# Layer norm and second norm: 1 / rms kept in the PSUM banks of its sums, Newton step in place, EPS added to the sum of squares

## The chip, the cores and the metric

The kernel runs on one core of one Trainium2 chip. The metric is the device time of one execution in microseconds (us); several runs are compared by their median. All times here are from the hardware profile of one execution or from those runs. The engines are named as the profile names them: PE (TensorE, the matmuls), DVE (VectorE), ACT (ScalarE), POOL (GpSimd) and SP (the queue that issues the loads).

## The reference, cut to what matters

One layer over 1088 tokens (1024 of a prompt, 64 of a decode step), 1024 channels, all float32. The change is in the layer norm inside it and in the second RMS norm:

```python
def layernorm(x, g, b):
    xf = x.astype(jnp.float32)
    mu = jnp.mean(xf, axis=-1, keepdims=True)
    xc = xf - mu
    var = jnp.mean(xc * xc, axis=-1, keepdims=True)
    r = xc * lax.rsqrt(var + EPS) * g.astype(jnp.float32) + b.astype(jnp.float32)
    return r.astype(x.dtype)

def layer(x, hist_a, hist_b, ...):
    h = rmsnorm(x, g_mix)
    z = jnp.einsum('btd,dc->btc', h, w_in)
    b_gate, c_gate, v, glu_val, glu_gate = jnp.split(z, 5, axis=-1)
    conv_a, new_a = causal_dwconv(c_gate * v, hist_a, conv_a_w)
    y_a = b_gate * conv_a
    u_b = glu_val * jax.nn.sigmoid(glu_gate)
    conv_b, new_b = causal_dwconv(u_b, hist_b, conv_b_w)
    y_b = jax.nn.silu(layernorm(conv_b + conv_b_bias, ln_b_g, ln_b_b))
    x = x + jnp.einsum('btc,cd->btd', jnp.concatenate([y_a, y_b], axis=-1), w_out)
    h2 = rmsnorm(x, g_ffn)
    f = jax.nn.silu(jnp.einsum('btd,df->btf', h2, w_gate)) * jnp.einsum('btd,df->btf', h2, w_up)
    x = x + jnp.einsum('btf,fd->btd', f, w_down)
    return x, new_a, new_b
```

## The kernel before

Channels lie on the 128 partitions and tokens on the free dimension. Each float32 matmul operand is split into two float16 parts (`high` L260 on ACT, `low` L263 on DVE or POOL; for weights `split_w`, L221 and L223 on ACT with L222 on POOL or L224 on DVE), and each product is three float16 matmuls (L247). Work is recorded as a list of tasks, each of which is a matmul group into two PSUM banks and its evacuation. Every engine runs its own instructions strictly in the order in which the recording wrote them, so an instruction that waits holds up everything behind it on its engine.

From about 225 us to 375 us of the span the kernel goes through these tasks:

- the last input projection tasks. The gate of group A is evacuated by L828, then split by L260 and L263; its convolution sums are made on POOL by L819.
- `layer_norm`, for two halves s of the tokens (every tile is 128x544: 2 x 272 tokens). L865 to L867 add up the four channel blocks. Matmuls with a matrix of ones (`column_sums`, L272) put the column sums into the PSUM tile `stat`, on every partition. L876 subtracts the mean, L878 squares, L880 adds the squares, and L272 sums again. Then `rstd_steps`: y0 on ACT (L289), m = mean square + EPS on ACT (L290), and three DVE instructions of one Newton step (L293, L294, L295). L896 multiplies the four blocks by the result r, L897 applies silu, L898 and L903 split.
- `out_task`: the output projection, 8 column blocks b for s = 0 and 8 for s = 1, evacuated into the residual `xt` by L942. L959 squares the result on ACT and L964 adds the squares.
- `second_norm`: for each s column sums (L272), y0, m and Newton as above, then eight products with r (L1003), each split by L260 and L263 into operands of the gate and up projections.
- gate and up projections (L1128 and L1131 evacuate the first ones). The first sums of weights for Strassen's scheme (L412, L413, L419, L423) are made on POOL.

PSUM in this stretch: three pairs of banks for products, and one pair, `stat`, that the six column sums use one after the other. r, m, y0 and t1 are tiles of the pool `sm` (11 buffers, names with s).

What the page calls L247 <-u,v or <-u,whl in this stretch are the output projection and the gate and up projections. w_o and w_gu are loads of weights that SP issues (L206) once their buffer is free.

Of the kernel before, what the change touches and what calls it, by code (L numbers as in the profile page):

```python
# [9 lines left out]
AF = mybir.ActivationFunctionType  # L10
ALU = mybir.AluOpType

P = 128
D = 1024
KB = D // P
GW = 512
# [12 lines left out]
EPS = 1e-6  # L29
# [6 lines left out]
ASC = 4.0  # L36
# [81 lines left out]
def halves(ap):  # L118

    return ap.rearrange("p (h w) -> p h w", h=2)  # L120


def quarter(ap, s):

    return halves(ap)[:, :, s * CW : (s + 1) * CW]
# [3 lines left out]
def trunk(ctx, tc, x, par, sta, stb, w_in, w_o, w_gu, w_ds, w_dl, y, st_out):  # L129
    nc = tc.nc  # L130
    pe, act, dve, gps = nc.tensor, nc.scalar, nc.vector, nc.gpsimd
# [15 lines left out]
    def nm(s):  # L147
        cnt[0] += 1
        return f"{s}{cnt[0]}"

    def unit(shape, dt=F32):
        return upool.tile(shape, dt, tag="u", name=nm("u"))
# [5 lines left out]
    def small():  # L158
        return sm.tile([P, HT], F32, tag="s", name=nm("s"))
# [10 lines left out]
    def begin(name, turns):  # L170

        cut_banks(part_b, "b", "ps_" + name)
        psum["phase"], psum["turns"], psum["n"] = name, turns, 0
# [16 lines left out]
    def stat_banks():  # L190
        if psum["phase"] == "rest":
            return bank2()
        if psum["phase"] == "first":
            return psum["b"].tile([P, 1, 512], F32, tag="stat", name=nm("stat"), bufs=2)
        return psum["b"].tile([P, 2, 512], F32, tag="stat", name=nm("stat"))

    def prm(i):
        return par_t[:, i : i + 1]
# [66 lines left out]
    def column_sums(parts):  # L265

        st = stat_banks()
        if len(parts[0].shape) == 3:
            n = parts[0].shape[2]
            for h in range(2):  # L270
                for i, p in enumerate(parts):
                    pe.matmul(  # L272
                        st[:, h, :n], ones, p[:, h], start=i == 0, stop=i == len(parts) - 1
                    )
            return st[:, :, :n]
        n = parts[0].shape[1]
        for i, p in enumerate(parts):
            pe.matmul(st[:, 0, :n], ones, p, start=i == 0, stop=i == len(parts) - 1)
        return st[:, 0, :n]

    def like(ap, t):

        return t[:, : ap.shape[1]] if len(ap.shape) == 2 else halves(t[:, : 2 * ap.shape[2]])

    def rstd_steps(sums, inv_n, scale, tiles=None):


        m, y0, t1, r = tiles or (like(sums, small()) for _ in range(4))
        act.activation(y0, sums, AF.Abs_reciprocal_sqrt, bias=epst[:, 0:1], scale=inv_n)  # L289
        act.activation(m, sums, AF.Identity, bias=epst[:, 0:1], scale=inv_n)  # L290

        def newton():
            dve.scalar_tensor_tensor(t1, m, -0.5 * scale, y0, ALU.mult, ALU.mult)  # L293
            dve.tensor_tensor(t1, t1, y0, ALU.mult)  # L294
            dve.scalar_tensor_tensor(r, t1, 1.5 * scale, y0, ALU.add, ALU.mult)  # L295
            return r

        return newton

    def rstd_of(sums, inv_n, scale):  # L300
        return rstd_steps(sums, inv_n, scale)()


    xt = cst.tile([P, KB, T], F32, name="xt")
# [32 lines left out]
    def run(steps):  # L337
        for _ in steps:
            pass
# [6 lines left out]
    for s, b in [(0, b) for b in range(KB)] + [(1, b) for b in ORDER1]:  # L346
# [5 lines left out]
        r, o, e = len(raws) - 1, (b % 2) * 1024, len(entries)  # L352
# [35 lines left out]
    scaled, loaded, sums = set(), {}, {}  # L388
# [449 lines left out]
    for j in range(NJ):  # L838
        for q, hf in TRIPLE:
# [3 lines left out]
                lambda acc, j=j, hf=hf, fn=fn: fn(acc, j, hf),  # L843
# [7 lines left out]
    def layer_norm():  # L851
        run(taps.steps)
        run(staps.steps)
        for j in range(NJ):
            act.activation(
                cb[j][:, TP:].rearrange("p (b t) -> p b t", b=SB),
                sacc[:, j],
                AF.Identity,
                bias=prm(PBI + j),
            )  # L860
        yb.extend(unit([P, 2, T], F16) for _ in range(NJ))
        for s in range(2):
            c = [quarter(b, s) for b in cb]
            tot = halves(small())
            dve.tensor_tensor(tot, c[0], c[1], ALU.add)  # L865
            dve.tensor_tensor(tot, tot, c[2], ALU.add)
            dve.tensor_tensor(tot, tot, c[3], ALU.add)  # L867
            got = []

            def first(tot=tot, s=s, c=c, got=got):  # L870
                if s == 0:
                    begin("out", "aab")
                mean = column_sums([tot])
                sq = []
                for j in range(NJ):
                    dve.scalar_tensor_tensor(c[j], mean, -1.0 / GW, c[j], ALU.mult, ALU.add)  # L876
                    sq.append(halves(small()))
                    act.activation(sq[j], c[j], AF.Square)  # L878
                for j in range(1, NJ):
                    dve.tensor_tensor(sq[0], sq[0], sq[j], ALU.add)  # L880
                got.append(sq[0])

            midway.append((PART1[s], first))
            while len(got) < 1:
                yield

            def second(got=got):
                got.append(rstd_steps(column_sums(got), 1.0 / GW, 1.0))

            midway.append((PART2[s], second))  # L890
            while len(got) < 2:
                yield
            r = got[1]()
            hl = [[quarter(yb[j][:, i], s) for i in range(2)] for j in range(NJ)]
            for j in range(NJ):
                dve.tensor_tensor(c[j], c[j], r, ALU.mult)  # L896
                act.activation(c[j], c[j], AF.Silu, scale=prm(PLG + j), bias=prm(PLB + j))  # L897
                act.activation(hl[j][0], c[j], AF.Copy, scale=ASC)  # L898
                if j == 1:
                    yield  # L900
            yield
            for j in range(NJ):
                dve.scalar_tensor_tensor(hl[j][1], c[j], ASC, hl[j][0], ALU.mult, ALU.subtract)  # L903
            ln_done.add(s)
            yield
# [5 lines left out]
    def out_task(b, s, *bg, part=None):  # L911
# [28 lines left out]
        def post(acc):  # L940
            o = quarter(xt[:, b], s)
            dve.scalar_tensor_tensor(o, acc[:, :, :CW], IN_SC, o, ALU.mult, ALU.add)  # L942
            return add_square((1, s), b, s)
# [9 lines left out]
    ssum, rstd2 = {}, {}  # L953
    ops = {}

    def add_square(key, b, s):

        sq = halves(small())
        act.activation(sq, quarter(xt[:, b], s), AF.Square)  # L959
        if key not in ssum:  # L960
            ssum[key] = sq
            return None
        o = ssum[key]
        return lambda: dve.tensor_tensor(o, o, sq, ALU.add) and None  # L964

    def operand(name, kp):

# [4 lines left out]
    def put(name, u, s, t):  # L972
        hl = [quarter(ops[name][u][:, i], s) for i in range(2)]
        high(hl[0], t)
        pend.append((hl[1], t, hl[0]))

    def settle(n):
        while len(pend) > n:
            low(*pend.pop(0))
# [3 lines left out]
    def second_norm(s):  # L983

        got = []


        def sums():
            got.append(rstd_steps(column_sums([ssum[1, s]]), 1.0 / D, ASC))

        midway.append((PART3, sums))
        while not got:
            yield
        r = got[0]()
        for name in ("B11", "B12", "B21", "B22"):
            if name not in ops:
                ops[name] = [unit([P, 2, T], F16) for _ in range(2)]
        for u in range(2):
            for q in range(2):
                tq = tqs[s, u, q] = (unit if (s, u, q) == (0, 0, 0) else unit_v)([P, 2, 2, CW])  # L1000
                for kk in range(2):
                    k = 4 * q + 2 * u + kk
                    dve.scalar_tensor_tensor(  # L1003
                        tq[:, kk], quarter(xt[:, k], s), prm(PG2 + k), r, ALU.mult, ALU.mult
                    )
                for hf in range(2):
                    put(f"B{q + 1}{hf + 1}", u, s, tq[:, :, hf])
                settle(2)
                yield
        settle(0)  # L1010
        yield
# [492 lines left out]
```

## Time and profile before

| | |
|---|---|
| median of 3 runs | 1020.53 us (1019.23 to 1020.68) |
| time of the profiled execution | 1019.75 us |
| its span in the profile | 1018.0 us |
| PE busy | 986.4 us (97%) |
| DVE busy | 761.1 us (75%) |
| ACT busy | 385.8 us (38%) |
| POOL busy | 340.6 us (33%) |

The span is the time from the first to the last recorded instruction; the 1.75 us beside it are outside the records. PE is nearly always busy, so a change can move the end only where PE stands still, or by work that PE does. The granted clock of TensorE was 0.996 of full speed over the span.

### The profile page before, as it was taken

Reading aid. Unit: us, or ns where it says so; the run is one execution under the profiler, and the core shown is the slowest. Engines: PE = TensorE matmul, PEld = TensorE weight load, DVE = VectorE, ACT = ScalarE, POOL = GpSimd, SP = SyncE. Lnnn points to the kernel's source line nnn. Section 1 sums busy time; section 2 is a strip of 40 time slices with the busy share of each in tenths; the row PEclk is TensorE's granted clock in tenths of the full one; section 3 lists DMA queues with packets and bytes.
Section 4 is the critical chain, followed back from the end, with each engine's and each line's share of the span. In section 5 each row is a group of like instructions: output and inputs, shape, how many; then the busy total and the mean of one; then the engine's idle time right before and its main releaser. Section 6 shows DMA issues by size and latency. Waiting matters only on the chain.

```text
span 1018.0 us, 19624 instructions
## 1 busy us (share of the span) xinstructions
PE 986.4 (97%) x8482; PEld 829.8 (82%) x8482; DVE 761.1 (75%) x1067; ACT 385.8 (38%) x692; POOL 340.6 (33%) x279
## 2 busy tenths in 40 slices
PE   5999999999899999999999999999999999999995
PEld 4788888888788878888888888888888888888884
DVE  7949999997677678987776767777676677755548
ACT  6611133237463534443322444332244333223332
POOL 3487854544000015323133322323422413240033
PEclk9999999999999999999999999999999999999998
DMA  9021111111410111121112112011211101211104
GB/s 345 32 83 43 42 43 53 42 43 53 166 42 1 43 42 42 43 73 33 36 69 84 43 42 73 32 62 46 80 43 53 62 32 63 82 44 42 42 1 176
DMA packets 17031, 63.01 MB, mean 62 GB/s; under 512 B 1169, under 2 KB 8481, under 8 KB 12081
## 3 DMA queue, kind: packets, MB, share of 16 engines
q1 hardware_dynamic: 16896, 61.67, 17.4%
q8 instruction: 66, 1.08, 0.5%
q14 instruction: 21, 0.16, 0.1%
q0 software_dynamic: 48, 0.09, 0.0%
HBM read 56.71 MB, written 5.05 MB: 61 GB/s over the span
## 4 chain that ended last, share of the span: by engine, by line
PE 68%; DVE 25%; ACT 3%; issue 2%; DMA 1%; POOL 0%; DVEq 0%; ACTq 0%
PE two L247 63%; DVE cv L548 12%; PE one L247 4%; DVE xt L1371 1%; DVE whl L224 1%; DVE u L263 1%; DVE v L1003 1%; DMA wf<-w_o 1%; DVE s L295 1%; PE stat L272 1%; DVE h L263 1%; DVE s L294 1%; DVE cv L543 1%; DVE v L263 1%; DVE xt L1319 0%
## 5 line engine op out<-in xcount | busy, mean ns | idle before, releaser
L247 PEld LDWEIGHTS <-whl 128*128 128x128 f16 x7464 | 730.2, 98 | 140.1 <-issue 4.5
L247 PE MATMUL two<-u,whl 128*128 128x272 f16 x4416 | 523.7, 279 | 3.8 <-DVE u L263 2.9
L247 PE MATMUL two<-h,whl 128*128 128x272 f16 x1512 | 186.1, 279 | 0.0
L247 PE MATMUL two<-v,whl 128*128 128x272 f16 x1536 | 178.5, 279 | 0.0
L423 POOL TENSOR_TENSOR s<-wf,s 128x512 f32<-128x512 f32 (+1 forms) x32 | 46.9, 1467 | 382.0 <-DVE whl L224 382.0
L223 ACT ACTIVATE whl<-wf 128x512 f16<-128x512 f32 (+1 forms) x150 | 87.6, 589 | 143.0 <-PE two L247 141.0
L548 DVE SCALAR_TENSOR_TENSOR cv<-u,par_t,cv 128x1024 f32<-128x1024 f32 x116 | 139.7, 1281 | 0.0
L224 DVE SCALAR_TENSOR_TENSOR whl<-wf,whl 128x512 f16<-128x512 f32 (+1 forms) x150 | 112.3, 765 | 1.2 <-ACT whl L223 1.2
L1278 DVE SCALAR_TENSOR_TENSOR xt<-two,xt 128x544 f32<-128x544 f32 x108 | 75.7, 719 | 41.0 <-PE two L247 40.4
L1169 DVE SCALAR_TENSOR_TENSOR s<-two,s 128x544 f32<-128x544 f32 x40 | 28.9, 723 | 66.1 <-PE two L247 66.1
L412 POOL TENSOR_TENSOR s<-wf 128x512 f32<-128x512 f32 (+1 forms) x32 | 40.6, 1270 | 111.8 <-DVE u L263 97.5
L223 ACT ACTIVATE whl<-s 128x512 f16<-128x512 f32 (+1 forms) x96 | 55.4, 583 | 59.5 <-PE two L247 55.8
L224 DVE SCALAR_TENSOR_TENSOR whl<-s,whl 128x512 f16<-128x512 f32 (+1 forms) x96 | 65.5, 696 | 0.0
L247 PE MATMUL two<-u,v 128*128 128x272 f16 x480 | 56.3, 279 | 1.9 <-DVE xt L942 1.9
L247 PEld LDWEIGHTS <-v 128*128 128x128 f16 x480 | 47.0, 98 | 11.1 <-issue 2.1
L260 ACT ACTIVATE h<-s 128x544 f16<-128x544 f32 x52 | 34.0, 657 | 52.8 <-DVE s L1162 48.1
L247 PE MATMUL one<-v,u 128*128 128x272 f16 (+2 forms) x480 | 49.2, 267 | 1.9 <-DVE v L263 1.8
L247 PEld LDWEIGHTS <-u 128*128 128x128 f16 x480 | 42.8, 104 | 8.7 <-issue 2.6
L1203 DVE SCALAR_TENSOR_TENSOR s<-two,s 128x544 f32<-128x544 f32 x20 | 14.5, 724 | 45.2 <-PE two L247 45.2
L222 POOL TENSOR_TENSOR whl<-wf,whl 128x512 f16<-128x512 f32 x38 | 44.1, 1187 | 10.1 <-ACT whl L221 10.0
L419 POOL TENSOR_TENSOR wf<-wf 128x512 f32<-128x512 f32 (+1 forms) x32 | 46.6, 1457 | 0.0
L413 POOL TENSOR_TENSOR s<-s,wf 128x512 f32<-128x512 f32 (+1 forms) x32 | 41.5, 1296 | 2.5
(127 smaller groups left out, 749.8 us busy)
## 6 DMA issues: line engine op xcount, KB each, us to landing
wf<-w_gu SPq DMA_DIRECT2D x22, 1024.0 KB, 4.9
wf<-w_ds SPq DMA_DIRECT2D x12, 768.0 KB, 4.2
wf<-w_in SPq DMA_DIRECT2D x8, 1024.0 KB, 5.1
wf<-w_o SPq DMA_DIRECT2D x6, 1024.0 KB, 5.3
xt<-x SPq DMA_DIRECT2D x3, 1088.0 KB, 11.3
y<-xt SPq DMA_DIRECT2D x2, 1088.0 KB, 5.1
u<-w_in SPq DMA_DIRECT2D x4, 512.0 KB, 7.7
wf<-w_dl SPq DMA_DIRECT2D x2, 1024.0 KB, 4.8
```

The source lines that it names most:

```text
L222: return whl, lambda: gps.tensor_tensor(lo, wf, hi, ALU.subtract) and None
L223: act.activation(hi, wf, AF.Copy, scale=WSC)
L224: return whl, lambda: dve.scalar_tensor_tensor(lo, wf, WSC, hi, ALU.mult, ALU.subtract) and None
L247: pe.matmul(out, w_[:, wpart, col : col + P], hl[:, apart, t0 : t0 + out.shape[1]], start=first and (i, q) == one, stop=last and (i, q) == ...
L260: act.activation(hi, tmp, AF.Copy)
L263: eng.tensor_tensor(lo, tmp, hi, ALU.subtract)
L412: gps.tensor_tensor(s1, a21, a22, ALU.add)
L413: gps.tensor_tensor(s2, s1, a11, ALU.subtract)
L419: gps.tensor_tensor(a21, a11, a21, ALU.subtract)
L423: gps.tensor_tensor(src, a12, src, ALU.subtract)
L548: dve.scalar_tensor_tensor(o_, i_, w, c, ALU.mult, ALU.add)
L1278: dve.scalar_tensor_tensor(o, bk[a_][:, :, :CW], IN_SC, o, ALU.mult, ALU.add)
```

## The change: what it does

`rstd_steps` is still there for the final norm. The layer norm and the second norm, in both halves, call a new function `rstd_kept`. It has one ACT instruction, y0 from the raw sums (the scale 1/n is in the activation), and no m. The Newton step runs on the PSUM tile of the sums, in place, and r stays there: `stat` is held until the last product with r. EPS no longer enters with y0 and m; it is added, times n / 128, to the partial sums of squares by the first of the adds, which becomes a scalar_tensor_tensor in place of a tensor_tensor (`add_with`).

```diff
-    def rstd_of(sums, inv_n, scale):
-        return rstd_steps(sums, inv_n, scale)()
+    def rstd_kept(sums, inv_n, scale):
+
+        y0 = like(sums, small())
+        act.activation(y0, sums, AF.Abs_reciprocal_sqrt, scale=inv_n)
+
+        def newton():
+            dve.scalar_tensor_tensor(sums, sums, -0.5 * scale * inv_n, y0, ALU.mult, ALU.mult)
+            dve.tensor_tensor(sums, sums, y0, ALU.mult)
+            dve.scalar_tensor_tensor(sums, sums, 1.5 * scale, y0, ALU.add, ALU.mult)
+            return sums
+
+        return newton
+
+    def add_with(eps, o, sq):
+
+        if eps:
+            dve.scalar_tensor_tensor(o, o, eps, sq, ALU.add, ALU.add)
+        else:
+            dve.tensor_tensor(o, o, sq, ALU.add)
...
-                    dve.tensor_tensor(sq[0], sq[0], sq[j], ALU.add)
+                    add_with(EPS * GW / P if j == 1 else None, sq[0], sq[j])
...
-                got.append(rstd_steps(column_sums(got), 1.0 / GW, 1.0))
+                got.append(rstd_kept(column_sums(got), 1.0 / GW, 1.0))
...
-            ssum[key] = sq
+            ssum[key] = sq, []
             return None
-        o = ssum[key]
-        return lambda: dve.tensor_tensor(o, o, sq, ALU.add) and None
+        o, others = ssum[key]
+        others.append(b)
+        eps = EPS * D / P if len(others) == 1 else None
+        return lambda: add_with(eps, o, sq)
...
-            got.append(rstd_steps(column_sums([ssum[1, s]]), 1.0 / D, ASC))
+            got.append(rstd_kept(column_sums([ssum[1, s][0]]), 1.0 / D, ASC))
```

In the changed kernel the lines are numbered 17 to 19 higher behind the new functions: L293 to L295 become L306 to L308, L289 becomes L303, L828 L845, L896 L913, L897 L914, L942 L959, L1003 L1022, L412 L429, L413 L430, L419 L436; the adds of squares L880 and L964 become L316 (the first of each row of adds, with EPS) and L318.

On DVE, at the layer norm of half 0, before (u are the channel blocks, s the tiles of the pool `sm`, two a product in PSUM; the numbers are those of the recording):

```order
L293 SCALAR_TENSOR_TENSOR s_2862<-s_2860,s_2861 128x544
L294 TENSOR_TENSOR s_2862<-s_2862,s_2861 128x544
L295 SCALAR_TENSOR_TENSOR s_2863<-s_2862,s_2861 128x544
L896 TENSOR_TENSOR u_1771<-u_1771,s_2863 128x2x272
L896 TENSOR_TENSOR u_1773<-u_1773,s_2863 128x2x272
L828 SCALAR_TENSOR_TENSOR s_2808<-two_2908,s_2808 128x544
```

and the same place now:

```order
L306 SCALAR_TENSOR_TENSOR stat_2857<-stat_2857,s_2860 128x2x272
L307 TENSOR_TENSOR stat_2857<-stat_2857,s_2860 128x2x272
L308 SCALAR_TENSOR_TENSOR stat_2857<-stat_2857,s_2860 128x2x272
L913 TENSOR_TENSOR u_1771<-u_1771,stat_2857 128x2x272
L913 TENSOR_TENSOR u_1773<-u_1773,stat_2857 128x2x272
L845 SCALAR_TENSOR_TENSOR s_2808<-two_2904,s_2808 128x544
```

No instruction of DVE changed its place; each of these now reads one tile from PSUM and one from SBUF, where it read two from SBUF.

On POOL, behind the last layer norm work, before (the sums of weights for Strassen's scheme, with the engines and queues whose counts each waits for):

```order
L222 TENSOR_TENSOR v_3024<-wf_2600,v_3024 128x1024 [waits DMAHW3_49,DVE_49,Activation_49]
L412 TENSOR_TENSOR s_4383<-wf_3993 128x512 [waits DVE_49,DMAHW6_49,PE_49,Pool_49]
L413 TENSOR_TENSOR s_4384<-s_4383,wf_3993 128x512 [waits DVE_49,PE_49,Pool_49]
L419 TENSOR_TENSOR wf_3993<-wf_3993 128x512 [waits DMAHW4_49,DMAHW2_49,DMAHW0_49]
L423 TENSOR_TENSOR s_4384<-wf_3993,s_4384 128x512 [waits DVE_49,Activation_49]
```

and now:

```order
L222 TENSOR_TENSOR v_3020<-wf_2600,v_3020 128x1024 [waits DMAHW3_49,DVE_49,Activation_49]
L429 TENSOR_TENSOR s_4367<-wf_3981 128x512 [waits DMAHW6_49,DVE_49,Activation_49]
L430 TENSOR_TENSOR s_4368<-s_4367,wf_3981 128x512 [waits PE_49,Pool_49]
L436 TENSOR_TENSOR wf_3981<-wf_3981 128x512 [waits DMAHW4_49,DMAHW2_49,DMAHW0_49]
L440 TENSOR_TENSOR s_4368<-wf_3981,s_4368 128x512 [waits DVE_49,Activation_49]
```

The order is the same, but with three tiles fewer for each norm the buffers of the pool `sm` go round differently. Before, L412 waits on DVE for an L263 just ahead of L293 of the second norm's half 1, and L413 for that L293. Now L429 waits on DVE for the last add of squares (L318), which stands four instructions earlier, and L430 for the column sums on PE.

On ACT each of the four norms loses the second activation; at the layer norm of half 0, before:

```order
L289 ACT_TABLE_LOAD
L289 ACTIVATE s_2861<-stat_2857,epst 128x544
L290 ACTIVATE s_2860<-stat_2857,epst 128x544
L585 COPY u_1179<-u_2656 128x2
L585 COPY u_1179<-v_97 128x16
```

and now:

```order
L303 ACT_TABLE_LOAD
L303 ACTIVATE s_2860<-stat_2857 128x544
L602 COPY u_1179<-u_2656 128x2
L602 COPY u_1179<-v_97 128x16
L827 ACTIVATE s_2878<-u_2656,par_t 128x480
```

All behind it on ACT stands one instruction earlier; PE and SP have the same instructions in the same order.

## Rows read from the trace of the kernel before

**Rows 1.** Waits of PE, whole span: us in total, times, longest us

```profile
PE two L247 <- DVE u L263: 2.9, 3, 1.6
PE two L247 <- DVE xt L942: 1.9, 1, 1.9
```

**Rows 2.** Timeline of PE, 220 to 300: start us, us, what, idle before

```profile
248.42 7.03 PE L247 MATMUL two<-u,whl 128*128 128x272 f16 x57
256.36 10.24 PE L247 MATMUL two<-u,whl 128*128 128x272 f16 x87 [0.92 <-DVE u L263]
268.48 10.12 PE L247 MATMUL two<-u,v 128*128 128x272 f16 x86 [1.88 <-DVE xt L942]
279.17 1.18 PE L272 MATMUL stat<-s,ones 128*128 128x272 f32 x4 [0.57 <-DVE s L867]
```

**Rows 3.** Timeline of PE, 343 to 374

```profile
363.29 7.00 PE L247 MATMUL two<-u,whl 128*128 128x272 f16 x58 [0.36 <-DVE whl L224]
371.87 0.28 PE L247 MATMUL two<-u,whl 128*128 128x272 f16 x1 [1.58 <-DVE u L263]
372.51 1.67 PE L247 MATMUL two<-u,whl 128*128 128x272 f16 x13 [0.36 <-DVE u L263]
```

**Rows 4.** Chain that ended last, 215 to 390: start us, us, what

```profile
239.81 0.61 ACT s L290
...
245.09 1.76 DVE u L896
...
255.82 2.50 POOL v L222
...
258.34 5.93 DMA wf<-w_o
...
267.71 0.73 DVE xt L942
```

**Rows 5.** Timeline of DVE, 236 to 257

```profile
240.45 1.23 DVE L293 SCALAR_TENSOR_TENSOR s<-s,s 128x544 f32<-128x544 f32 x1 [2.09 <-ACT s L290]
241.72 1.57 DVE L294 TENSOR_TENSOR s<-s,s 128x544 f32<-128x544 f32 x1
243.32 1.74 DVE L295 SCALAR_TENSOR_TENSOR s<-s,s 128x544 f32<-128x544 f32 x1
...
252.09 0.72 DVE L828 SCALAR_TENSOR_TENSOR s<-two,s 128x544 f32<-128x544 f32 x1
```

**Rows 6.** Timeline of ACT, 220 to 300

```profile
243.10 1.28 ACT L897 ACT_TABLE_LOAD   x1
246.87 0.84 ACT L897 ACTIVATE u<-u,par_t 128x544 f32<-128x544 f32 x1 [2.49 <-DVE u L896]
```

**Rows 7.** Timelines of POOL, 200 to 300 and 300 to 400

```profile
242.66 3.59 POOL L819 TENSOR_TENSOR s<-s,s 128x544 f32<-128x544 f32 x2
...
355.77 1.53 POOL L412 TENSOR_TENSOR s<-wf 128x512 f32<-128x512 f32 x1 [97.46 <-DVE u L263]
```

**Rows 8.** Lines L876, L548 (ns min/median/max); stretches: PE, PEld, DVE, ACT, POOL busy

```profile
L876 DVE SCALAR_TENSOR_TENSOR u<-stat,u x8: 711/714/724, 230.1 to 282.8; 128x544 f32<-128x544 f32 x8
...
L548 DVE SCALAR_TENSOR_TENSOR cv<-u,par_t,cv x116: 1275/1280/1285, 70.3 to 223.0; 128x1024 f32<-128x1024 f32 x116
...
70.00:223.00 153.00, 153.00 (x1322) 129.19 (x1321) 153.00 (x146) 39.68 (x80) 98.61 (x84) 1.00 0.13 44
...
280.30:363.00 82.70, 82.54 (x699) 68.97 (x696) 61.67 (x90) 39.80 (x60) 4.87 (x3) 1.00 0.08 27
```

**Rows 9.** Timeline of DVE, 346 to 374

```profile
354.82 0.72 DVE L263 TENSOR_TENSOR u<-s,u 128x544 f16<-128x544 f32 x1 [3.26 <-ACT u L260]
...
356.21 1.68 DVE L294 TENSOR_TENSOR s<-s,s 128x544 f32<-128x544 f32 x1
...
359.63 2.37 DVE L1003 SCALAR_TENSOR_TENSOR v<-xt,par_t,s 128x544 f32<-128x544 f32 x2
...
371.11 1.34 DVE L263 TENSOR_TENSOR u<-v,u 128x544 f16<-128x544 f32 x2
```

## The prediction

> **What bounds the kernel now.** First I read which engine is never idle: PE is busy 97% of the span, so the end moves only where PE stands still. Then the waits of PE [rows 1]: three waits for L263 and one for L942 are 4.8 us. The timelines of PE say where. In the first place, around the layer norm of half 0, PE stands still 0.92 us before 256.36, 1.88 us before 268.48 and 0.57 us before 279.17 [rows 2], 3.37 us together. In the second, around the second norm of half 1, it is 0.36, 1.58 and 0.36 us [rows 3], 2.30 us together. Between the places PE has no gap worth naming: 82.54 of 82.70 us busy [rows 8]. So this change can give back some 5.7 us at most, and it can only lose where it makes a gap.
>
> Third, the chain of waits says what those gaps wait for. Its pieces in the first place run through the Newton step and its first product, L896 at 245.09, to ACT (silu and splits), POOL's L222 at 255.82, the load of w_o that waits for L222 to free its buffer (258.34), and DVE's L942 at 267.71 [rows 4], which frees the bank that PE waits for at 268.48. So it is one chain from the norm to PE: what the norm ends earlier, PE gets earlier, until its gaps are used up.
>
> Fourth, the Newton steps themselves. Half 0 of the layer norm takes 1.23, 1.57 and 1.74 us for its three instructions of 128x544 [rows 5], where an instruction of this size with two inputs in SBUF takes 0.72 undisturbed (L263) [rows 9]. POOL runs beside them: its two L819 from 242.66 take 3.59 us [rows 7]. In the second norm of half 1 it is the same: L294 takes 1.68 us from 356.21, two L1003 take 2.37 us [rows 9], and POOL's L412 starts at 355.77 [rows 7]. All these DVE instructions read two tiles from SBUF.
>
> **What the change takes away.** *One activation for each norm*: DVE starts its Newton step when L290 ends; now it starts when L289 does, 0.61 us earlier [rows 4], and all behind it on ACT is that much earlier too. *The slow steps*: no row of before has a DVE instruction that reads and writes `stat` in place. From below, L876, which reads `stat` and a tile in SBUF, takes 0.714 us [rows 8]. From above, with POOL beside it, the slowest step is 1.74 us [rows 5]. I take 0.75 us for each step (0.71 and 0.04 us until the next, dependent one starts; L294 starts 0.04 us after L293 ends [rows 5]) and 0.71 for a product with r. The nearest row for such an instruction beside a busy POOL is L548: PSUM and SBUF in, PSUM out, 116 times, 1275 to 1285 ns, in a stretch in which POOL is busy 98.61 of 153 us [rows 8]. A spread of 10 ns leaves no room for a neighbour.
>
> [...]
>
> *EPS* turns the first of each row of adds from a tensor_tensor into a scalar_tensor_tensor of the same shape and operands. Undisturbed, one of the first kind takes 0.72 us (L263) [rows 9] and one of the second 0.714 (L876) [rows 8], so it costs nothing.
>
> **First place, worked out.** DVE starts at 240.45 - 0.61 = 239.84. Three steps at 0.75 and the first product at 0.71 end at 242.8; before it was 245.09 + 1.76 = 246.85 [rows 4]. ACT needs a table load ahead of silu, 1.28 us from 243.10 [rows 6], now from 242.49 to 243.77. So L897 starts at 243.8 in place of 246.87: the Newton step is then hidden by the table load, and ACT is 3.07 us earlier. The evacuation L828 that ACT's next split needs started at 252.09 [rows 5] and would now stand at 249.0; it needs products that PE ends as it starts the next operand at 248.42 [rows 2], so it still does not wait. L222 on POOL, the load and L942 follow 3.07 us earlier. L942 would end at 267.71 + 0.73 - 3.07 = 265.4. PE, without the 0.92 us, gets there at 268.48 - 1.88 - 0.92 = 265.7: both gaps are gone, the second by 0.3 us only. At 279.17 the gap waits for DVE's L867, which stands behind those L942: 276.10. PE alone would be there at 279.17 - 3.37 = 275.8. So PE is 3.07 us earlier from there on, and 0.3 us of gap stays.
>
> **The two norms in between** (layer norm half 1, second norm half 0) lose the same work and give nothing: the 82.54 busy us of PE cover it [rows 8]. If that cover were gone, each would be worth its 0.61 us.
>
> **Second place.** ACT's L260 ahead of L263 comes 0.61 us earlier, and DVE stands idle for it (3.26 us, until 354.82) [rows 9]. L294, L295 and the first two products took from 356.21 to 362.00 [rows 9], 5.79 us; at 0.75 each it is 3.0. Together 3.4 us. The L224 behind them frees PE's 0.36 us, and the two L263 at 371.11 start at 367.7 and end by 369.1. Without its gaps PE needs them at 371.87 - 1.58 - 0.36 = 369.9. All 2.30 us go, with 0.8 us to spare. POOL's sums move as well: L412 now waits for an add that stands ahead of the idle stretch, which began at 351.56. It therefore runs beside idle DVE. If it should still hold up the three DVE instructions ahead of that stretch, there are 3.26 - 0.61 = 2.65 us of idle time to take it.
>
> **`stat` held longer.** The next sums into it come at 279.17 [rows 2], 27 us behind the L828 at 252.09 [rows 5], which stands behind the last product of half 0 on DVE. PE, on which they would hold up all products behind them, does not wait for the bank.
>
> **The sum**: 3.07 + 2.30 = 5.4 us. The profiled execution took 1019.75 us (span 1018.0), so 1014.4, with a span of 1012.6. The median of the runs is 0.78 above the profiled execution; from it, **1015.1 us**. Its own range: 4.6 us of gain, if 0.8 us of the margins above fail, to 5.7 if the last 0.3 goes as well: 1014.8 to 1015.9, and with the 0.7 us by which the three runs scatter, 1014.2 to 1016.6.
>
> [...]
>
> **The rivals.**
>
> *POOL goes on slowing the steps* (what they contend for is not the second read of SBUF): then the first place gains the 0.61 us of the activation, and the second still 2.30, since POOL moves away in time. 2.9 us, **1017.6**. For it: no row has an in-place step of this form. Against it: L548. 15%.
>
> *The second place gives nothing*: POOL's sums, now earlier, hold up L263 and the adds ahead of it by more than the idle time takes, and DVE comes as late as before. 3.1 us of gain, **1017.5**. Against it: the three sums take about 1.5 us each (L412) [rows 7], and DVE's idle time takes more than half of that. 9%.
>
> *No change that can be told*: it does not do what it says, because the gaps open elsewhere. The buffers of `sm` go round differently, so waits have moved, and PE comes earlier to all that follows. For it: DVE is busy 61.67 of 82.70 us even between the places [rows 8]. Against it: that leaves 21 us to make up 3. 8%, **1020.5**.
>
> *Slower*: a step that reads and writes the same PSUM tile right behind another costs far more than one into SBUF. It decides from (246.85 - 239.84) / 4 = 1.75 us an instruction: above this L896 ends later than before. At 2.1 us, the first place loses 1.4 us; in the second, 0.61 us are won and the five instructions from 355.5 take 10.5 us where they took 6.5, 3.4 lost: **1025**. Against it: L548 rewrites its PSUM tile too, 1024 wide, in 1.28 us. 4%.
>
> **How the numbers follow.** The forecast has 64%. About 0.2% (2 us) is what a measurement of this kernel can tell from no change, so all below 1018.5 is faster: 64 + 15 + 9 = 88%, of which I take 1 for mishaps of both kinds: 87, 8, 5. The range of 8 in 10 takes the forecast and the two rivals of half the gain: 1013.9 to 1018.2.
>
> **What would show it.** Right: `stat` steps of 0.7 to 0.8 us while POOL is busy; the first silu near 243.8; no PE gap near 255.4 and 265.7, at most 0.4 near 276; L429 on POOL near 347; no gaps of PE near 360 and 367; span near 1012.6. Wrong: steps above 1 us; L942 still ahead of a PE gap though all before it is early, which would mean that the load has another release; or a new gap of PE behind 372.

## The result and the profile after

The changed kernel takes 1012.9 us (median of 4 runs, 1012.53 to 1014.15), the kernel before 1020.04 beside it (4 runs, 1019.23 to 1020.68). The ratio is 0.9934, with a 95% interval of 0.9922 to 0.9946: by it 6.7 us less (5.5 to 8.0). The forecast was 1015.1 and its range began at 1013.9, so the sign and the places were right and the gain was too small, by 1.0 us more than the range allowed. The profiled execution has a span of 1010.8 us (before 1018.0) and took 1013.21 us (before 1019.75). Of all executions one stands apart, of the second norm alone, with 5170.71 us at a granted clock of 0.19, and its ratio leaves it out.

The timeline of PE in the changed kernel, first place (start us, us, what it did, idle time before it and what ended that). Rows of before: [rows 2].

```profile
228.10 1.19 PE L272 MATMUL stat<-s,ones 128*128 128x272 f32 x4 [0.94 <-DVE s L884]
...
247.65 16.84 PE L247 MATMUL two<-u,whl 128*128 128x272 f16 x144
264.33 10.12 PE L247 MATMUL two<-u,v 128*128 128x272 f16 x86
274.43 1.19 PE L272 MATMUL stat<-s,ones 128*128 128x272 f32 x4
```

All three gaps are gone, the one at 279.17 too, of which 0.3 us was forecast to stay. From 248.42 to 279.17 it was 30.75 us before; from 247.65 to 274.43, the same 230 matmuls, it is now 26.78. The place gives 3.97 us; 3.07 was forecast, and [rows 2] show only 3.37 us of idle time. PE is 0.77 us earlier at 247.65 already, ahead of all that the change touches (the experiments come back to that).

The same view, second place; of before [rows 3].

```profile
344.96 1.19 PE L272 MATMUL stat<-s,ones 128*128 128x272 f32 x4
345.98 19.04 PE L247 MATMUL two<-u,whl 128*128 128x272 f16 x163
365.27 48.46 PE L247 MATMUL two<-u,whl 128*128 128x272 f16 x417 [0.25 <-DVE u L263]
```

Of three gaps, one of 0.25 us is left, ahead of the matmul that stood at 372.51. In the profile of before, the L272 of this place starts at 349.70: 22.81 us to there before, 20.31 now, so the place gives 2.50 us. The earlier start and the two places are 0.77 + 3.97 + 2.50 = 7.24 us, all of the 7.2 by which the spans differ. One of the forecast's signs of being wrong, a new gap of PE behind the second place, is there: 0.24 us, behind the 417 matmuls of the last row. It costs little: from 372.51 to 441.06 before, 585 matmuls, is 68.55 us, and the same stretch now, from 365.27 to 433.91, is 68.64.

The timeline of DVE, both norms; of before [rows 5] and [rows 9].

```profile
238.98 0.73 DVE L306 SCALAR_TENSOR_TENSOR stat<-stat,s 128x544 f32<-128x544 f32 x1 [1.39 <-ACT s L303]
239.75 0.73 DVE L307 TENSOR_TENSOR stat<-stat,s 128x544 f32<-128x544 f32 x1
240.52 0.73 DVE L308 SCALAR_TENSOR_TENSOR stat<-stat,s 128x544 f32<-128x544 f32 x1
241.29 1.35 DVE L913 TENSOR_TENSOR u<-u,stat 128x544 f32<-128x544 f32 x2
...
344.82 0.72 DVE L1043 TENSOR_TENSOR s<-v,s 128x544 f32<-128x544 f32 x1
345.46 0.72 DVE L263 TENSOR_TENSOR u<-s,u 128x544 f16<-128x544 f32 x1
346.09 0.72 DVE L1043 TENSOR_TENSOR s<-v,s 128x544 f32<-128x544 f32 x1
349.38 1.72 DVE L263 TENSOR_TENSOR u<-s,u 128x544 f16<-128x544 f32 x1 [2.57 <-ACT u L260]
351.02 0.72 DVE L306 SCALAR_TENSOR_TENSOR stat<-stat,s 128x544 f32<-128x544 f32 x1
351.78 0.73 DVE L307 TENSOR_TENSOR stat<-stat,s 128x544 f32<-128x544 f32 x1
352.55 0.73 DVE L308 SCALAR_TENSOR_TENSOR stat<-stat,s 128x544 f32<-128x544 f32 x1
353.31 1.47 DVE L1022 SCALAR_TENSOR_TENSOR v<-xt,par_t,stat 128x544 f32<-128x544 f32 x2
```

Each step takes 0.73 us and the next follows 0.77 us after its start (0.75 was forecast; before 1.23 to 1.74). One thing is worse: the L263 at 349.38 takes 1.72 us, where before it took 0.72 at 354.82. The timeline of POOL says why; of before [rows 7].

```profile
239.16 2.28 POOL L222 TENSOR_TENSOR whl<-wf,whl 128x512 f16<-128x512 f32 x2
241.39 2.78 POOL L836 TENSOR_TENSOR s<-s,s 128x544 f32<-128x544 f32 x2
...
251.88 2.48 POOL L222 TENSOR_TENSOR v<-wf,v 128x1024 f16<-128x1024 f32 x1 [2.64 <-ACT v L221]
...
345.04 2.90 POOL L429 TENSOR_TENSOR s<-wf 128x512 f32<-128x512 f32 x1 [90.68 <-DVE s L318]
348.02 1.27 POOL L430 TENSOR_TENSOR s<-s,wf 128x512 f32<-128x512 f32 x1
349.25 1.27 POOL L436 TENSOR_TENSOR wf<-wf 128x512 f32<-128x512 f32 x1
```

In the first place POOL is busy beside all three steps, and neither engine is slowed (the two sums of L836 take 2.78 us, before 3.59). In the second, L429 starts at 345.04 and takes 2.90 us, beside the three DVE instructions with two inputs in SBUF that last until 346.81, and so L436 comes to lie beside the L263 at 349.38.

The timeline of ACT, ahead of the silu; of before [rows 6].

```profile
241.64 1.28 ACT L914 ACT_TABLE_LOAD   x1
242.93 0.84 ACT L914 ACTIVATE u<-u,par_t 128x544 f32<-128x544 f32 x1
```

The silu follows the table load at once, where before it waited 2.49 us for DVE. And the waits of PE's products (L247 into `two`) that are left (us in total, times, longest us); of before [rows 1].

```profile
PE two L247 <- DVE s L1188: 0.6, 2, 0.3
PE two L247 <- DVE u L263: 0.2, 1, 0.2
```

The lines of DVE that the change touches (busy us, mean ns of one):

```profile
L318 DVE TENSOR_TENSOR s<-s,s 128x544 f32<-128x544 f32 x16 | 11.5, 721 | 1.5 <-ACT s L976 1.1
...
L913 DVE TENSOR_TENSOR u<-u,stat 128x544 f32<-128x544 f32 x8 | 5.4, 715 | 0.1
...
L316 DVE SCALAR_TENSOR_TENSOR s<-s,s 128x544 f32<-128x544 f32 x4 | 2.9, 720 | 0.7 <-ACT s L976 0.7
```

EPS costs nothing: an add with it takes 720 ns (L316), one without 721 (L318). The product with r from PSUM takes 715.

### The profile page after: what moved, and what is told of

Same layout as the page of the kernel before. It is cut to its first block, busy times and chain, and to the rows that moved or that the text cites. A ratio compares the mean times of both kernels' runs of the same rounds, so it can differ in the third digit from the quotient of the medians.

```text
span 1010.8 us, 19618 instructions
## 1 busy us (share of the span) xinstructions
PE 984.8 (97%) x8482; PEld 829.2 (82%) x8482; DVE 755.0 (75%) x1067; ACT 383.1 (38%) x688; POOL 339.9 (34%) x279
## 4 chain that ended last, share of the span: by engine, by line
PE 73%; DVE 23%; issue 2%; ACT 1%; DMA 0%; DVEq 0%; ACTq 0%
PE two L247 68%; DVE cv L565 12%; PE one L247 4%; DVE xt L1390 1%; DVE u L263 1%; DVE whl L224 1%; PE stat L272 1%; DVE v L1022 1%; DVE h L263 1%; DVE cv L560 1%; DVE v L263 1%; DVE xt L1338 1%; DVE s L681 0%; DMA xt<-x 0%; DVE s L845 0%
## 5 line engine op out<-in xcount | busy, mean ns | idle before, releaser
L247 PEld LDWEIGHTS <-whl 128*128 128x128 f16 x7464 | 730.3, 98 | 136.3 <-issue 1.3
L247 PE MATMUL two<-u,whl 128*128 128x272 f16 x4416 | 522.9, 279 | 0.8 <-DVE s L1188 0.6
L247 PE MATMUL two<-h,whl 128*128 128x272 f16 x1512 | 186.1, 279 | 0.0
L247 PE MATMUL two<-v,whl 128*128 128x272 f16 x1536 | 178.5, 279 | 0.0
L1188 DVE SCALAR_TENSOR_TENSOR s<-two,s 128x544 f32<-128x544 f32 x40 | 28.9, 723 | 66.1 <-PE two L247 66.1
L429 POOL TENSOR_TENSOR s<-wf 128x512 f32<-128x512 f32 (+1 forms) x32 | 42.1, 1316 | 105.5 <-DVE s L318 90.7
L247 PE MATMUL two<-u,v 128*128 128x272 f16 x480 | 56.3, 279 | 0.0
L247 PEld LDWEIGHTS <-v 128*128 128x128 f16 x480 | 47.0, 98 | 9.0
L247 PE MATMUL one<-v,u 128*128 128x272 f16 (+2 forms) x480 | 48.5, 264 | 1.9 <-DVE v L263 1.8
L247 PEld LDWEIGHTS <-u 128*128 128x128 f16 x480 | 42.1, 102 | 8.7 <-issue 2.6
L222 POOL TENSOR_TENSOR whl<-wf,whl 128x512 f16<-128x512 f32 x38 | 43.6, 1171 | 8.3 <-ACT whl L221 8.2
L436 POOL TENSOR_TENSOR wf<-wf 128x512 f32<-128x512 f32 (+1 forms) x32 | 46.2, 1443 | 0.0
L430 POOL TENSOR_TENSOR s<-s,wf 128x512 f32<-128x512 f32 (+1 forms) x32 | 41.1, 1285 | 2.5
```

Of the source, the lines that this page charges most:

```text
L222: return whl, lambda: gps.tensor_tensor(lo, wf, hi, ALU.subtract) and None
L247: pe.matmul(out, w_[:, wpart, col : col + P], hl[:, apart, t0 : t0 + out.shape[1]], start=first and (i, q) == one, stop=last and (i, q) == ...
L429: gps.tensor_tensor(s1, a21, a22, ALU.add)
L430: gps.tensor_tensor(s2, s1, a11, ALU.subtract)
L436: gps.tensor_tensor(a21, a11, a21, ALU.subtract)
```

## Experiments

Each was timed in five rounds. The first four ran on one chip, beside 15 runs of the kernel before with a median of 1019.46 us; the next four on another, beside 19 with 1019.57; the last beside 9 with 1020.47. None leaves out work. Gains at the two places are read from PE's timelines as above, against 30.75 and 22.81 us.

**Layer norm alone.** The second norm goes back to the old steps in SBUF.

```diff
-        eps = EPS * D / P if len(others) == 1 else None
+        eps = None
...
-            got.append(rstd_kept(column_sums([ssum[1, s][0]]), 1.0 / D, ASC))
+            got.append(rstd_steps(column_sums([ssum[1, s][0]]), 1.0 / D, ASC))
```

> Only the layer norm keeps 1 / rms in its banks; the second norm is as before. If each place gives its own gaps back (theory: the steps were slow because POOL read SBUF beside them), the first place is worth 3.1 to 4.0 us and the second place keeps its gaps of 0.36, 1.58 and 0.36 us: 1016.0 to 1017.0, ratio 0.996 to 0.997. If the whole gain came from something outside the norms (the start of the program, the load), the time is that of the changed kernel, near 1013, or of the kernel before, near 1020.

Measured: 1016.16 us, ratio 0.9966 (0.9954 to 0.9978). The first place gives 4.10 us (248.35 to 275.00), the second nothing: its gaps are 0.37, 1.58 and 0.36 us. The time is as expected, and the place gives the 3.1 to 4.0 us that were expected, and 0.1 more; in the profile 1.7 us are lost again behind the second place, to PE's clock (last section). The median lies where no run does: four runs took 1014.86 to 1015.27 us and four, the profiled one among them, 1017.05 to 1017.70.

**Second norm alone.** The layer norm goes back.

```diff
-                    add_with(EPS * GW / P if j == 1 else None, sq[0], sq[j])
+                    add_with(None, sq[0], sq[j])
...
-                got.append(rstd_kept(column_sums(got), 1.0 / GW, 1.0))
+                got.append(rstd_steps(column_sums(got), 1.0 / GW, 1.0))
```

> Only the second norm keeps 1 / rms in its banks; the layer norm is as before. By the theory the second place is worth 2.3 to 2.5 us and the first keeps its gaps of 0.92, 1.88 and 0.57: 1017.5 to 1017.8, ratio 0.9975. If the gaps open elsewhere, within 1 us of before.

Measured: 1016.81 us, ratio 0.9973 (0.9962 to 0.9984), 0.7 us under what was expected, of which 0.6 is the base: the kernel before took 1019.46 us beside it and 1020.04 beside the first result. The second place gives 2.50 us (349.10 to 369.41), the first 0.40: its gaps stay, 0.91, 1.48 and 0.57 us, and in the second of them the load of w_o is 0.4 us shorter than before. So the two halves work apart from one another, and neither takes the other's gain.

**The activation gone, the steps in SBUF.** Only the first step reads PSUM; t1 and r are tiles in SBUF again.

```diff
+        t1, out = (like(sums, small()) for _ in range(2))
...
+            dve.scalar_tensor_tensor(t1, sums, -0.5 * scale * inv_n, y0, ALU.mult, ALU.mult)
+            dve.tensor_tensor(t1, t1, y0, ALU.mult)
+            dve.scalar_tensor_tensor(out, t1, 1.5 * scale, y0, ALU.add, ALU.mult)
+            return out
```

> All four norms without the second activation and with EPS in the sum of squares, but t1 and r lie in SBUF as before: only the first step reads PSUM. If the steps are slow because both their inputs lie in SBUF beside a busy POOL, the second and third step and the first products stay slow (1.2 to 1.7 us), the first place gains 0.6 of the activation and 0.5 of the first step, 1.1 us, the second 0.6: 1018.3, ratio 0.998. If it is the activation that counted, near 1014.

Measured: 1016.63 us, ratio 0.997 (0.9958 to 0.9982), 1.7 us under what was expected, 0.6 of it the base and the rest from the second place. The timeline of DVE in the first place:

```profile
238.99 0.72 DVE L308 SCALAR_TENSOR_TENSOR s<-stat,s 128x544 f32<-128x544 f32 x1 [1.40 <-ACT s L303]
239.74 1.17 DVE L309 TENSOR_TENSOR s<-s,s 128x544 f32<-128x544 f32 x1
240.95 1.56 DVE L310 SCALAR_TENSOR_TENSOR s<-s,s 128x544 f32<-128x544 f32 x1
242.54 3.53 DVE L915 TENSOR_TENSOR u<-u,s 128x544 f32<-128x544 f32 x2
```

The step with one input in PSUM takes 0.72 us, the next ones, with two in SBUF, 1.17, 1.56 and 1.77 each: in one norm, behind one another, beside the same POOL. The place gives 1.09 us, as expected. The second gives 1.90 (347.85 to 368.76), where 0.6 was expected, and that is not the steps: they take 0.72, 1.36 and 1.67 us there. It is POOL, whose first sum waits for another tile in this kernel's order of buffers and starts at 349.15, in DVE's idle time, so that the L263 at 352.27 takes 0.73 us.

**The steps in PSUM, the activation kept.** ACT scales the sums in place.

```diff
+        act.activation(sums, sums, AF.Identity, scale=inv_n)
...
-            dve.scalar_tensor_tensor(sums, sums, -0.5 * scale * inv_n, y0, ALU.mult, ALU.mult)
+            dve.scalar_tensor_tensor(sums, sums, -0.5 * scale, y0, ALU.mult, ALU.mult)
```

> All four norms with the second activation, which writes m into the banks of the sums in place, and Newton in PSUM. By the theory of the port the steps take 0.73 us and nearly all is gained: 0.6 us less than the changed kernel in the first place and at most 0.6 in the second, 1013.5 to 1014.5, ratio 0.994 to 0.995. If it is the activation that counted, near 1019.

Measured: 1013.55 us, ratio 0.9939 (0.9927 to 0.9951), as expected. That a port is what the two engines share, no run shows; the 0.73 us is the step measured in the changed kernel. The timeline of DVE in the first place:

```profile
239.45 0.73 DVE L308 SCALAR_TENSOR_TENSOR stat<-stat,s 128x544 f32<-128x544 f32 x1 [1.91 <-ACT stat L305]
240.22 0.73 DVE L309 TENSOR_TENSOR stat<-stat,s 128x544 f32<-128x544 f32 x1
240.99 0.73 DVE L310 SCALAR_TENSOR_TENSOR stat<-stat,s 128x544 f32<-128x544 f32 x1
```

The steps take 0.73 us; the first place gives 3.43 us (247.61 to 274.93, with one gap of 0.52), the second 2.50. So the operands in PSUM are nearly the whole gain, and the activation alone is worth 0.5 us, in the first place.

**The changed kernel once more.** Not edited.

> The changed kernel once more, unedited. Between the two profiles, PE is 0.77 us earlier at 22 us already, ahead of every norm: 81 matmuls from 14.5 us took 7.57 us before and 6.89 after. Theory: that is scatter of the start and not of the change, since kernels that keep half of the change show 7.41, 7.24, 6.92 and 6.83; then this profile shows any value from 6.8 to 7.6 for them, and the first L272 behind them anywhere from 228.0 to 228.9. Rival: the change itself does it, then 6.9 and 228.1 again within 0.1. Time 1012.5 to 1014.2 by both. The gap of PE at 264 stays away if the load of w_o was not lucky; if its 5.9 us of waiting was, a gap of up to 0.5 us comes back at 274.

Measured: 1012.94 us (5 runs, 1012.84 to 1013.62), ratio 0.9932 (0.9919 to 0.9944). The 81 matmuls take 7.05 us and the first L272 starts at 228.39, 0.29 later than in the first profile of the same kernel: the start scatters, and over all eleven profiles here the 81 take 6.29 (POOL's sums later, below) to 7.57. The 7.57 is the one profile of the kernel before, so whether that kernel scatters as much is not shown. The places give 4.11 us (247.94 to 274.58) and 2.49 (345.00 to 365.32), no gap at 264 or 274.

**POOL's sums later.** Two small tiles, touched by POOL ahead of and behind S1 and S2, move the buffers on, so that S1 waits for a later reader.

```diff
         if name == "S2":
+            held = [small(), small()]
+            for h in held:
+                gps.memset(h[:, :1], 0.0)
             s1, s2 = (small()[:, :n] for _ in range(2))
...
             gps.tensor_tensor(s2, s1, a11, ALU.subtract)
+            for h in held:
+                gps.memset(h[:, :1], 0.0)
```

> The changed kernel, with two more small tiles held by POOL ahead of its sums S1 and S2 in the second norm of half 1 (each touched in one column by a memset, twice), so that S1 waits for the L263 at 345.5 instead of the L318 at 344.2, and S2 for the L263 at 349.4. Theory (only DVE instructions with two inputs in SBUF are slowed by POOL and slow it): the L263 at 349.4 takes 0.72 in place of 1.72 us; POOL's S2 and S3 now run beside the three steps in PSUM, which stay at 0.73 us, and take 1.27 us each; the 0.25 us gap of PE at 365 goes. Gain 0.4 us: 1012.2 to 1012.8. Rival (the steps were quick in this place only because POOL was done): steps of 1.2 to 1.7 us, S2 of 1.7 us, the gap at 365 grows to about 1 us, and the time to 1013.5 to 1014.

Measured: 1018.93 us, ratio 0.9988 (0.9978 to 0.9999): 6 us slower than the changed kernel, by neither theory. The timelines of DVE and POOL in the second place:

```profile
349.02 0.73 DVE L263 TENSOR_TENSOR u<-s,u 128x544 f16<-128x544 f32 x1 [2.57 <-ACT u L260]
349.66 0.72 DVE L306 SCALAR_TENSOR_TENSOR stat<-stat,s 128x544 f32<-128x544 f32 x1
350.42 0.73 DVE L307 TENSOR_TENSOR stat<-stat,s 128x544 f32<-128x544 f32 x1
351.19 0.73 DVE L308 SCALAR_TENSOR_TENSOR stat<-stat,s 128x544 f32<-128x544 f32 x1
```

```profile
345.94 1.64 POOL L432 TENSOR_TENSOR s<-wf 128x512 f32<-128x512 f32 x1
349.89 1.28 POOL L433 TENSOR_TENSOR s<-s,wf 128x512 f32<-128x512 f32 x1 [2.31 <-DVE u L263]
...
351.20 1.27 POOL L441 TENSOR_TENSOR wf<-wf 128x512 f32<-128x512 f32 x1
```

In the place itself all is as the theory of the two SBUF inputs has it: the L263 takes 0.73 us, POOL's sums run beside the steps, and neither is slowed; PE's gap is gone. But the edit moved POOL's sums in all groups behind it too, and there they met other instructions. The groups of DVE's combining adds in this kernel, and the waits of PE (us in total, times, longest us):

```profile
L1111 DVE TENSOR_TENSOR s<-s,s 128x544 f32<-128x544 f32 x8 | 10.6, 1320 | 0.3
...
L1112 DVE TENSOR_TENSOR s<-s,s 128x544 f32<-128x544 f32 x8 | 8.9, 1118 | 0.0
```

```profile
PE two L247 <- DVE s L1193: 6.6, 6, 1.3
```

The same adds take 724 and 718 ns in the changed kernel, and PE's waits for this line (L1188 there) are 0.6 us in 2 times. So that theory held, and the expectation fell because it looked at one place. That the longer adds bring PE's waits rests on the edit that takes both away again (the last experiment).

**The final norm in PSUM too.** Two steps in place, the third into an SBUF tile, which POOL then multiplies by; EPS in the add of block 6.

```diff
-            dve.scalar_tensor_tensor(sums, sums, 1.5 * scale, y0, ALU.add, ALU.mult)
-            return sums
+            r = sums if out is None else like(sums, out)
+            dve.scalar_tensor_tensor(r, sums, 1.5 * scale, y0, ALU.add, ALU.mult)
+            return r
...
+            if b == SQ_POOL:
+                return lambda: add_with(EPS * D / P, c, sq)
...
-            got.append(rstd_steps(st, 1.0 / D, 1.0))
+            got.append(rstd_kept(st, 1.0 / D, 1.0, small()))
```

> The changed kernel, with the final norm in the same form too: no activation for m, EPS in its sum of squares (in the add of block 6), two steps in place in PSUM and the third from PSUM into an SBUF tile, because POOL multiplies by it. POOL is idle there, so the steps themselves gain nothing (0.44 us each either way); the activation of 0.48 us lies on the path at the tail. Expected: from PE's last sums to the first product behind the norm 3.96 us now, 3.6 then; time 0.4 us less, 1012.2 to 1013. Rival: the tail is set by the loads of y or by POOL's two products of 0.95 us, and nothing moves: 1012.6 to 1013.2.

Measured: 1011.39 us, ratio 0.9916 (0.9903 to 0.993): 1.5 us less than the changed kernel, where 0.4 was expected. From PE's last sums to the first product behind the norm it is 3.51 us (998.70 to 1002.21), 3.96 in the changed kernel: 0.45 less, as expected. The rest is earlier: the norm of the first half, too, has lost its activation and a step slowed by POOL (1.17 to 0.73 us), DVE's products behind it come 0.9 us earlier, and PE no longer waits for an add that stood among them:

```profile
989.87 1.08 PE L278 MATMUL two<-s,ones 128*128 128x272 f32 x4
990.79 7.69 PE L247 MATMUL two<-h,whl 128*128 128x272 f16 x65
998.70 1.60 PE L278 MATMUL two<-s,ones 128*128 128x272 f32 x4 [0.21 <-DVE s L317]
```

In the changed kernel these stand at 990.23, behind a gap of 0.29, at 991.66 and at 999.75. The expectation had looked only at the tail, where POOL is idle (4.78 us ahead of its product at 1003.82), and not at the first half, where it is busy (a sum of 0.98 us from 980.71, beside the step of 1.17).

**Both.** The two edits together.

> The late sums of POOL and the final norm in PSUM together. Theory: 0.4 us at 365 and 0.4 us at the tail, 1011.8 to 1012.4. Rival: each moves nothing or trades its gain away, 1012.6 to 1013.5.

Measured: 1018.01 us, ratio 0.9975 (0.9966 to 0.9985), by neither. PE waits the same 6.6 us in the later groups.

**Both, with the tiles held once.** As the last, with the two tiles held only ahead of the first S2, that of the second place.

```diff
+            held = [] if late_once else [small(), small()]
+            late_once.append(1)
```

> The changed kernel, the final norm in PSUM as in final_kept, and the two held tiles ahead of POOL's sums only the first time, in the second norm of half 1. Theory: what made pool_late slow is where POOL's later sums fell (the two adds of a group's combinations took 1.32 and 1.12 us on DVE in place of 0.72, and a PE gap of up to 1.29 us stood in each of the four later groups), so without the held tiles there the later gaps are as in the changed kernel, 0.6 us, and the gap at 365 is gone: 1010.9 to 1011.5, against 1011.39 of final_kept. Rival: two tiles taken once shift the ring of small tiles for good, and the gaps come as in pool_late: 1017 to 1018.5.

Measured: 1010.9 us, ratio 0.9904 (0.9888 to 0.992), as expected and the lowest median here. PE in the second place has no gap:

```profile
344.85 1.18 PE L272 MATMUL stat<-s,ones 128*128 128x272 f32 x4
345.87 32.36 PE L247 MATMUL two<-u,whl 128*128 128x272 f16 x278
```

PE's waits for the later groups are back at 0.5 us. The theory that only the place of POOL's sums had made the edit slow is borne out. Against 1011.39 of the final norm alone, on another chip, 0.5 us is no more than their runs scatter, so that this kernel is the faster of the two is not shown.

## Why the prediction was wrong in size

**The mechanism was right.** DVE's steps were slow because they had two inputs in SBUF while POOL ran beside them; the one kernel with a step of each kind (0.72, then 1.17 and 1.56) and the one with the activation kept (3.43 and 2.50 us at the two places) show it. The rival "POOL goes on slowing the steps" falls, and so do "slower", "no change" and, with 2.50 us, "the second place gives nothing". With one input in PSUM the steps of the first place take 0.73 us while POOL is busy without a break (239.16 to 244.17). Nor does the operand in PSUM make an instruction of this size longer by more than 0.01 us: 0.73 us against 0.72 for an L263, which has both inputs in SBUF [rows 9].

**How the two engines slow each other** the prediction worked out in one direction only, what POOL costs DVE. In the second place of the changed kernel, L429 takes 2.90 us where such a sum takes 1.27; the 1.63 us more are most of the 1.77 for which DVE's three instructions go on beside it (345.04 to 346.81), and these keep their 0.72. The L263 at 349.38, in turn, takes 1.72 us, 1.00 more than 0.72, and POOL's L436, at 1.27 not slowed, has 1.14 us to go when it starts. So in both cases here the instruction that starts second is longer by most of what is left of the other's work, and the one that started first is not. Where both have work one behind the other, as in the first place of before, both are longer (steps of 1.23 to 1.74 us, two L819 of 3.59); whether they take turns there or run side by side at a lower rate, these rows do not tell.

**The step that failed is "this change can give back some 5.7 us at most"**, and with it the two terms of the sum. The idle times in [rows 2] and [rows 3] were added up as if each were the time that PE loses. A row of a matmul lasts 279 ns in the profile, but in an unbroken stretch the next one starts after 26.78 / 230 = 0.116 us; idle time is counted from the end of the row, so a gap loses its idle time and 0.163 us more. By this, which is worked out from the rows, three gaps hide 0.49 us: the first place had some 3.86 us to lose, not 3.37, and the second 2.79, not 2.30. Measured between the same matmuls, it lost 3.97 and 2.91 (2.50 and the 0.41 of the gap that stays). The first term, forecast at 3.07, is 3.97 to 4.11 in the two profiles of the changed kernel; the second, forecast at 2.30, is 2.50.

**First place.** The start of DVE, the steps and the silu came where they were put: the forecast's 243.8 for the silu less the 0.77 us of the start is 243.03, and it starts at 242.93. The 0.3 us that were to stay at 279 went as well, because the load of w_o was taken over with the length it had before. From the end of POOL's L222 to the ACT instruction that waits for the load it was 6.04 us before (258.31 to 264.35) and is 5.24 after (254.36 to 259.60); the eight profiles of the changed kernel and of the experiments in which it starts by 255.1 have 4.84 to 5.25, the three (that of before with them) in which it starts later 5.65 to 6.37. What makes it longer there stays open.

**Second place.** "It therefore runs beside idle DVE" failed. L429 starts at 345.04 and takes 2.90 us beside DVE's two-input adds, not 1.5: the forecast priced what POOL could cost those adds, and not what they cost POOL. So the last sum lies beside the L263 that ends the idle stretch, which takes 1.72 us. A gap of 0.25 us stays, against which the forecast had given 0.8 us to spare. The kernel with POOL's sums moved shows that cause by taking it away: 0.73 us, and no gap.

**The base.** The forecast stood on 1020.53, the median of three runs. The 43 runs of the kernel before beside the experiments have a median of 1019.76, so 0.77 us of the miss is the base. From that median to the 1012.94 of the nine runs of the changed kernel it is 6.8 us. The places give 6.5 to 6.6. The time around the span, which the forecast kept at its 1.75 us, has grown from 1.77 to 2.34 (medians), a loss of 0.57; why, no view here shows. And the runs of before differ in their granted clock: the 12 with a mean of 0.997 have a median of 1018.96 us, the 6 with 0.993 one of 1022.34, while all nine of the changed kernel stand at 0.996 or 0.997. Against the 12, the gain is 6.02, which is the 6.6 less the 0.57. The other 0.8 goes with the clock. That the gaps cost it is likely from what follows, but not shown: no profile of before fell on it, and the earlier start (0.77 and 0.48 us in the two profiles of the changed kernel) may have a part in it. So the 2.2 us between the forecast and 1012.9 are 0.77 of base, 0.9 to 1.04 of the first place, 0.2 of the second and the 0.8 that goes with the clock, less the 0.57 around the span.

## What to carry to other kernels

In this kernel a two-input VectorE step of 128x544 beside a busy GpSimd came down from 1.23 to 1.74 us to 0.73 by keeping one operand in PSUM: look for all chains of small steps that have one there anyway, the last norm as well as the first. Measure what a gap of PE costs between the same two matmuls, not by the idle time in its row, and then ask what each gap's own waits (a load, a sum) will take at the new time. Where buffers of a ring decide when GpSimd runs, an edit at one place can move it in all later ones (two tiles held by POOL took DVE's later adds from 0.72 to 1.32 and 1.12 us): compare the groups of DVE that have two SBUF inputs over the whole span before blaming the place.

## What the hardware showed that was not expected

PE's granted clock falls to 0.50 behind the gaps of the second place in one of the two profiles that have all three of them. In the kernel with the layer norm alone, the stretches of PE behind the three gaps (us, PE busy, granted clock, DMA share, GB/s):

```profile
366.00:369.00 3.00, 1.07 (x6) 0.88 0.00 0
369.00:371.00 2.00, 2.00 (x11) 0.50 0.00 0
371.00:373.00 2.00, 2.00 (x16) 0.83 0.00 0
373.00:375.00 2.00, 2.00 (x20) 1.00 0.00 0
```

In the row at 0.50 PE does 11 matmuls in 2 us, in the row at 1.00 it does 20. The row of 417 matmuls that begins there is:

```profile
368.24 50.12 PE L247 MATMUL two<-u,whl 128*128 128x272 f16 x417 [0.36 <-DVE u L263]
```

The changed kernel does these 417 in 48.46 us, so in this profile PE loses 1.66 us behind the gaps, beside the gaps themselves. In the profile of before, with the same gaps, the clock stays at 1.00. What decides it is not shown, nor whether it parts the two groups of four runs of this kernel, which lie some 2.4 us apart.

At the start PE does 12 to 13 matmuls a microsecond from 17 us on and then 22, all at a granted clock of 1.00 in the rows; the step comes between 20 and 21 us in the profile of before and near 19 in that of after, and this is 0.68 of the 0.77 us between them (7.57 and 6.89 us for the 81 matmuls).
